# The cast ahead of a one-column product, placed earlier in a written order of the attention stage

## The chip, the cores and the metric

The kernel runs on one core of one Trainium2 chip. The metric is the device time of one execution in microseconds (us), as the median of several runs; lower is better. The engines of the core are TensorE (PE in the profile, its weight loads PEld), VectorE (DVE), ScalarE (ACT), GpSimd (POOL) and SyncE (SP), which here only issues DMAs. Each engine takes its own list of instructions in order; they meet through semaphores.

## What is computed

One layer of a decoder trunk on a sequence of 1024 positions with model width 1024, all in float32 at the interface. Cut to what matters:

```python
h = rms_norm(x, norm_mix_pre)
q, k, v, cb, cc, cx, g_att, g_conv = split(h @ w_in)       # 8 heads x 64, conv width 512
o = stick_breaking_attention(q, k, v)                      # strictly causal
y_att = o @ w_att_branch
y_conv = (cb * causal_dwconv(cc * cx, conv_mix_w)) @ w_conv_branch
merged = sigmoid(g_att) * y_att + sigmoid(g_conv) * y_conv
x = x + rms_norm(merged @ w_out, norm_mix_post)
h = rms_norm(x, norm_ffn_pre)
a, g = split(causal_dwconv(h @ w_up, conv_ffn_w))          # 2 x 2816
x = x + rms_norm((gelu(g) * a) @ w_down, norm_ffn_post)
```

The attention is, for each query t and key s < t, `w[t, s] = sigmoid(z[t, s]) * prod over s < j < t of (1 - sigmoid(z[t, j]))` with `z = q.k / 8`, and `o = w @ v`.

## The kernel before

**Products in halves.** Each operand of a large product is split into two float16 parts, a high one and the remainder, and three of the four partial products are accumulated (`PASSES`). Before it is split, an operand is scaled by a power of two that is taken from its mean square. That scale is made in these steps: ACT squares the tile and sums each partition (`sumsq`, L57); DVE casts the 128 sums to bfloat16 (`scale_sum`, L76, or L73 and L74 where several sums are added first); PE multiplies a matrix of ones with that one column (L79), which puts the total on all partitions; DVE turns the total into the power and its inverse with three integer operations (`scale_pow`, L86, L88, L89); ACT writes the high part (L192 or L96) and DVE the low part (L197 or L97).

**The stages.** After the normalisation and transposition of x come the products for v, q0 and k0, then the attention stage; then the rest of the branches, the gates, the output projection and the feed-forward part. The attention stage alone is written under a manual schedule for PE, ACT, DVE and SP: the instructions stand on each engine in the order in which the Python code issues them. The order of the other parts is planned by the compiler's own scheduler.

**The attention stage.** It walks over 24 units: four pairs of heads j, four pairs of query tiles p, and for p of 2 or 3 two ranges of keys. A unit is named j_p_first key tile (0_3_4 is j = 0, p = 3, keys from tile 4 on). Each unit has two halves, one per query tile, of a width W of 128 to 512 keys. For each half, in this order: PE makes the scores z (L510, with a mask product L514 in the range at the diagonal); ACT takes two sigmoids of them (`R` L518, `be` L519); ACT and DVE turn the weights of the half before into two float16 parts (L548, L550), which SP sends through a transposing DMA (L553); DVE runs two scans (L531) and the weighing (L540). At every second half PE also makes the weighted sums of the unit before the last one (`products`, L576).

Behind each half stands filler work for PE: 384 groups of three products of 512 columns, from v_tile (4 tiles of 8 groups), q and k of j + 1 (16 groups each, two half tiles of 8), the conv tiles (48 groups: cc, cx and cb), the two first gates (16 each) and four branch tiles (8 each). `run_fill` (in `mixer`) issues them up to a number that grows with the share of the attention that is done, some 10 groups behind a half of width 512, 7, 5 and 3 behind the narrower ones. The half tiles' PSUM comes from a pool of three buffers (`pm`), from which the one-column product takes its buffer too; the scores have two (`z`).

**The planned steps.** `plan_weight` hangs the steps of a weight's preparation on the filler's count: a step with `lead` stands so many groups ahead of the weight's first use `at`, but not ahead of its `floor`. `run_fill` calls the steps of a count just ahead of that group. Steps at count -1 are called ahead of all. In the kernel before, `total` holds both the cast and the one-column product; `split` holds the power and the high part; `low` the low part. `plan_p` does the same for the four tiles of the conv branch's product, whose squares are summed together. Weights are staged in four buffers (`ws`) from `fetch` to `low`.

Of the kernel before, what the change touches and what calls it, by code (L numbers as in the profile page):

```python
# [38 lines left out]
class Layer:  # L39
# [18 lines left out]

    def scale_of(self, sm, n, keep=False, slack=0):

        return self.scale_pow(*self.scale_sum(sm, n, keep), slack)

    def scale_sum(self, sm, n, keep=False):

        nc = self.nc
        if keep:
            r = self.const.tile([P, 4], F32, tag=f"sc{self.nsc}", name=f"sc{self.nsc}", bufs=1)
        else:
            r = self.smp.tile([P, 4], F32, tag="sc", name=f"sc{self.nsc}", bufs=16)
        self.nsc += 1  # L70
        rb = self.smp.tile([P, 1], BF16, tag="rb", name=f"rb{self.nsc}", bufs=8)
        if n > 1:
            nc.vector.tensor_reduce(r[:, 0:1], sm[:, 0:n], AX.X, ALU.add)  # L73
            nc.vector.tensor_copy(rb, r[:, 0:1])  # L74
        else:
            nc.vector.tensor_copy(rb, sm[:, 0:1])  # L76
        pool, shape, tag = self.sum_psum
        ps = pool.tile(shape, F32, tag=tag, name=f"pr{self.nsc}")
        nc.tensor.matmul(ps[:, 0:1], self.ones, rb, start=True, stop=True)  # L79
        return r, ps  # L80

    def scale_pow(self, r, ps, slack=0):
# [89 lines left out]
    def plan_weight(self, steps, name, at):  # L172

        nc = self.nc
        src = dict(self.wseq)[name][0]
        h = {}

        def fetch():
            h["sm"] = self.small(f"sm_{name}", w=8)
            h["t"] = self.ws.tile([P, D], F32, tag="ws", name=f"ws_{name}")  # L180
            nc.sync.dma_start(h["t"], src)

        def squares():
            self.sumsq(h["t"], h["sm"][:, 0:1], name)

        def total():
            h["r"], h["ps"] = self.scale_sum(h["sm"], 1)

        def split():
            h["s"], inv = self.scale_pow(h["r"], h["ps"])  # L190
            w = self.wh.tile([P, 2, D], F16, tag="wh", name=f"wh_{name}")
            nc.scalar.activation(w[:, 0, :], h["t"], AF.Copy, scale=h["s"])  # L192
            self.wdone[name] = [w], inv

        def low():
            w = self.wdone[name][0][0]
            nc.vector.scalar_tensor_tensor(w[:, 1, :], h["t"], h["s"], w[:, 0, :], ALU.mult, ALU.subtract)  # L197
        for f, lead, floor in ((fetch, 46, -1), (squares, 36, 5), (total, 30, 11), (split, 25, 15), (low, 21, 18)):
            steps.setdefault(max(floor, at - lead), []).append(f)

    def rstd_of(self, src, name):
# [108 lines left out]
    def mixer(self, mid):  # L310
        tc, nc, a = self.tc, self.nc, self.a
        hT = self.hp.tile([P, 2, KD, T], F16, tag="hT", name="hT")
        with ExitStack() as ph1:
# [66 lines left out]
            acts, inv_x = [None, o16], [None, inv_ov]  # L380
# [4 lines left out]
            smp_ = self.small("sm_p", keep=True)  # L385
# [50 lines left out]
            def plan_p(steps, at):  # L436

                h = {}
                acts[0] = []

                def total():
                    h["r"], h["ps"] = self.scale_sum(smp_, 4, keep=True)

                def power():
                    h["s"], inv_x[0] = self.scale_pow(h["r"], h["ps"])

                def part(j):
                    def f():
                        t = self.slot([P, 2, T], F16, f"p16_{j}")
                        self.split(t, pf[j], h["s"], f"p{j}")  # L450
                        acts[0].append(t)
                    return f
                for f, q in [(total, 5), (power, 10)] + [(part(j), 12 + 4 * j) for j in range(4)]:
                    steps.setdefault(at + q, []).append(f)

            sig = {}
# [36 lines left out]
            def units_of():  # L493

                for j in range(4):
                    for p in range(4):
                        for lo in ((512, 0) if p >= 2 else (0,)):
                            yield dict(j=j, p=p, lo=lo, nb=min(4, 2 * p + 2 - lo // P), nm=f"{j}_{p}_{lo // P}",
                                       top=lo > 0 or p < 2, end=lo == 0)

            def scores(u, tt, tl):

                j, i, lo, nm = u["j"], tt, u["lo"], f"{u['nm']}{tl}"
                s = stk[j]
                W = min(NH, (i + 1) * P - lo)
                z = pat.tile([P, 2, NH], F32, tag="z", name=f"z{nm}", bufs=2)
                for n, (hq, hk) in enumerate(PASSES):
                    for h in range(2):
                        d = ds(64 * h, 64)
                        nc.tensor.matmul(z[:, h, :W], s["q"][d, hq, ds(i * P, P)], s["k"][d, hk, ds(lo, W)],  # L510
                                         start=n == 0, stop=n == 2 and not u["top"], skip_group_check=True)
                if u["top"]:
                    for h in range(2):
                        nc.tensor.matmul(z[:, h, W - P:W], self.identb, self.maskb, start=False, stop=True,  # L514
                                         skip_group_check=True)
                R = att.tile([P, 2, NH + 1], F32, tag="R", name=f"R{nm}", bufs=4)
                be = att.tile([P, 2, NH], F32, tag="be", name=f"be{nm}", bufs=2)
                nc.scalar.activation(R[:, :, :W], z[:, :, :W], AF.Sigmoid, scale=s["cz"][1])  # L518
                nc.scalar.activation(be[:, :, :W], z[:, :, :W], AF.Sigmoid, scale=s["cz"][0])  # L519
                return dict(u=u, tl=tl, W=W, R=R, be=be, nm=nm)  # L520
# [16 lines left out]
            def weigh(t):  # L537

                W = t["W"]
                nc.vector.tensor_tensor(t["be"][:, :, :W], t["be"][:, :, :W], t["R"][:, :, 1:W + 1], ALU.mult)  # L540

            def turn(t, part):

                u, W, be = t["u"], t["W"], t["be"]
                w = t["R"].rearrange("p h s -> p (h s)").bitcast(F16)[:, :4 * W]
                wv = [w[:, ds(2 * W * hl, 2 * W)].rearrange("p (h s) -> p h s", h=2) for hl in range(2)]
                if part == 0:
                    nc.scalar.activation(wv[0], be[:, :, :W], AF.Copy)  # L548
                else:
                    nc.vector.tensor_tensor(wv[1], be[:, :, :W], wv[0], ALU.subtract)  # L550
                    if "wT" not in u:
                        u["wT"] = att.tile([P, 32, P], F16, tag="wT", name=f"wT{u['nm']}", bufs=2)
                    nc.sync.dma_start_transpose(u["wT"][:, ds(t["tl"] * 4 * u["nb"], 4 * W // P), :], w)  # L553
# [55 lines left out]
            def run_fill(upto):  # L609

                while state["done"] < upto:
                    for f in steps.pop(state["done"], ()):
                        f()
                    next(chained, None)
                    state["done"] += 1

            def attention():
                us = list(units_of())
                total = sum(3 * u["nb"] + 1 + (3 * min(u["nb"], 2 * u["p"] + 1 - u["lo"] // P) + 1) for u in us)
                seen, last = 0, None  # L620
                for f in steps.pop(-1, ()):
                    f()
                for k in range(len(us) + 2):
                    for tl in (1, 0):
                        if k < len(us):
                            u = us[k]
                            t = scores(u, 2 * u["p"] + tl, tl)
                            seen += 3 * (t["W"] // P) + 1
                        else:
                            t = None  # L630
                        if last is not None:
                            turn(last, 0)
                        if t is not None:
                            scan(t)
                        if last is not None:
                            turn(last, 1)
                        if t is not None:
                            weigh(t)
                        last = t
                        if tl == 0 and k >= 2:  # L640
                            products(us[k - 2])
                        run_fill(seen * (n_fill - 24) // total + 6 * max(0, 2 * (k - len(us)) + 2 - tl))
                run_fill(n_fill)
                next(chained, None)
# [566 lines left out]
```

## Time and profile before

| | |
|---|---|
| median of 3 runs | 1489.27 us (1488.35 to 1490.51) |
| profiled execution | 1490.44 us |
| span of its trace | 1488.5 us |
| mean granted TensorE clock over the span | 0.953 |
| PE busy | 1330.4 us |
| DVE busy | 1007.1 us |
| ACT busy | 804.4 us |
| attention stage: first scores to last filler group | 72.0 to 527.0 us |

The span runs from the first to the last instruction of the trace. Busy time is that of instructions; the end of a product on PE is modelled. In the profile's rows a line number such as L79 is the line of the kernel below, `out<-in` names the tiles, and `[3.82 <-DVE rb L76]` is idle time of the engine ahead of the instruction with what ended it. The granted clock is the share of TensorE's full clock that was granted in a stretch.

### The profile page before, as it was taken

What the parts mean: (1) busy time and instruction counts of PE and PEld (TensorE: products, weight loads), DVE (VectorE), ACT (ScalarE), POOL (GpSimd) and SP (SyncE); (2) the same over time, 40 slices, a digit from 0 to 9 for tenths busy, and PEclk for the clock granted to TensorE, in tenths of its full rate; (3) what the DMA queues carried; (4) which work ended last, traced back from release to release, by engine and by line L of the source; (5) the groups of instructions that cost most, each with busy time, mean ns of one, the idle gap of its engine ahead of it and who ended that gap; (6) DMA issues with size and microseconds to landing.
All of it is one profiled execution on the core that took longest, in us unless ns stands there. A gap on an engine that the chain in (4) does not pass through costs nothing. (4 is left out here: it accounts for less than half of the span.)

```text
span 1488.5 us, 16951 instructions
## 1 busy us (share of the span) xinstructions
PE 1330.4 (89%) x6543; PEld 600.0 (40%) x6543; DVE 1007.1 (68%) x1649; ACT 804.4 (54%) x1138; POOL 48.1 (3%) x69
## 2 busy tenths in 40 slices
PE   5978777788777887899999999999999999999997
PEld 3433333333333333344445444444444444444443
DVE  6455565566665419888778988596497388299848
ACT  6343444354444554656665647766576476376612
POOL 1000000000000000000001100001000100100001
PEclk9988888899888998999999999999999999999999
DMA  6022333333332401123324212515524713921315
GB/s 242 1 46 68 71 73 73 68 85 69 81 67 57 110 29 42 57 71 100 142 69 144 71 57 74 204 48 129 140 59 114 168 57 101 269 84 51 120 57 184
DMA packets 109392, 139.58 MB, mean 94 GB/s; under 512 B 79088, under 2 KB 79088, under 8 KB 109312
## 3 DMA queue, kind: packets, MB, share of 16 engines
q1 hardware_dynamic: 105360, 124.28, 27.9%
q0 software_dynamic: 3952, 14.23, 5.3%
q8 instruction: 51, 0.84, 0.2%
q14 instruction: 29, 0.24, 0.1%
HBM read 94.45 MB, written 25.17 MB: 80 GB/s over the span
## 5 line engine op out<-in xcount | busy, mean ns | idle before, releaser
L1081 PEld LDWEIGHTS <-wh_u 128*128 128x128 f16 x1848 | 178.8, 98 | 217.7 <-issue 4.0
L976 PE MATMUL pd<-wdh,f 128*128 128x512 f16 x1056 | 232.2, 381 | 10.3 <-DVE wdh L97 5.7
L976 PEld LDWEIGHTS <-f 128*128 128x128 f16 x1056 | 103.6, 98 | 137.4 <-issue 12.2
L79 PE MATMUL pr<-rb,ones 128*128 128x1 bf16 x75 | 11.9, 167 | 118.4 <-DVE rb L76 95.9
L518 ACT ACTIVATE R<-z,cz 128x1024 f32<-128x1024 f32 (+3 forms) x48 | 43.2, 899 | 114.8 <-PE z L514 59.9
L531 DVE TENSOR_TENSOR_SCAN R<-R,zero 128x256 f32<-128x256 f32 (+3 forms) x64 | 49.3, 811 | 68.0 <-ACT R L518 67.9
L1081 PEld LDWEIGHTS <-wh_g 128*128 128x128 f16 x588 | 57.0, 98 | 74.7 <-ACT hB L667 4.3
L791 PE MATMUL py<-wh_wo,m 128*128 128x512 f16 x384 | 83.9, 379 | 0.0
L97 DVE SCALAR_TENSOR_TENSOR wh_u<-ws_u,sc,wh_u 128x1024 f16<-128x1024 f32 (+1 forms) x66 | 72.2, 1102 | 8.9 <-ACT wh_u L96 8.9
L96 ACT ACTIVATE wh_u<-ws_u,sc 128x1024 f16<-128x1024 f32 (+1 forms) x66 | 64.2, 998 | 22.6 <-DVE ws_u L916 12.6
L980 ACT ACTIVATE y<-pd,sd 128x512 f32<-128x512 f32 x64 | 42.1, 692 | 58.2 <-PE pd L976 51.9
L531 DVE TENSOR_TENSOR_SCAN R<-R,cy,zero 128x512 f32<-128x512 f32 x32 | 39.4, 1272 | 40.0 <-ACT R L518 39.7
L86 DVE TENSOR_SCALAR sc<-pr 128x1 int32<-128x1 int32 x75 | 11.1, 154 | 77.0 <-PE pr L79 77.0
L1158 DVE SCALAR_TENSOR_TENSOR ugu<-cgu,cw_g,ugu 128x1023 f32<-128x1023 f32 (+1 forms) x44 | 56.3, 1280 | 10.1 <-ACT ugu L1156 10.0
L1158 DVE SCALAR_TENSOR_TENSOR ua<-cau,cw_a,ua 128x1023 f32<-128x1023 f32 (+1 forms) x44 | 56.3, 1279 | 2.0 <-ACT ua L1156 1.8
L791 PEld LDWEIGHTS <-m 128*128 128x128 f16 x384 | 37.5, 98 | 44.1
L242 PE MATMUL pcb<-hT,wh_cb 128*128 128x512 f16 x192 | 52.0, 429 | 0.0
L346 PE MATMUL pv<-wh_v,hT 128*128 128x512 f16 x192 | 48.8, 411 | 2.4 <-ACT wh_v L96 1.7
L242 PE MATMUL pcx<-hT,wh_cx 128*128 128x512 f16 x192 | 50.6, 420 | 0.0
L242 PE MATMUL pq<-hT,wh_q 128*128 128x512 f16 x192 | 48.5, 406 | 2.1 <-ACT hT L231 1.2
L242 PE MATMUL pcc<-hT,wh_cc 128*128 128x512 f16 x192 | 50.2, 420 | 0.0
L482 PE MATMUL pywa<-o,wh_wa 128*128 128x512 f16 x192 | 48.5, 416 | 1.9 <-ACT wh_wa L96 1.9
(610 smaller groups left out, 2585.0 us busy)
## 6 DMA issues: line engine op xcount, KB each, us to landing
ws_u<-w_up_nt SPq DMA_DIRECT2D x44, 512.0 KB, 3.5
yd<-y POOLq DMA_DIRECT2D x24, 512.0 KB, 5.4
ds<-w_down SPq DMA_DIRECT2D x22, 512.0 KB, 6.1
wd<-w_down SPq DMA_DIRECT2D x22, 512.0 KB, 3.5
ws_g<-w_in_nt SPq DMA_DIRECT2D x14, 512.0 KB, 3.6
x<-x SPq DMA_DIRECT2D x8, 512.0 KB, 8.1
ws_wo<-w_out SPq DMA_DIRECT2D x8, 512.0 KB, 6.4
xr<-x SPq DMA_DIRECT2D x8, 512.0 KB, 4.2
```

What stands on the lines that cost most here:

```text
L96: self.nc.scalar.activation(dst[:, 0, :], src, AF.Copy, scale=s)
L97: self.nc.vector.scalar_tensor_tensor(dst[:, 1, :], src, s, dst[:, 0, :], ALU.mult, ALU.subtract)
L242: nc.tensor.matmul(ps, w[:, wi, ds(k * P, P)], hT[:, hi, k, ds(c * NH, NH)], start=n == 0, stop=n == last)
L346: nc.tensor.matmul(pv, hT[:, hi, k, ds(tt * P, P)], wv[k // 2][:, wi, ds((k % 2) * NH, NH)], start=n == 0, stop=n == 3 * KD - 1)
L482: nc.tensor.matmul(ps, w[0][:, wi, ds((d % 2) * NH + k * P, P)], acts[bi][k][:, hi, ds(c * NH, NH)], start=n == 0, stop=n == 11)
L518: nc.scalar.activation(R[:, :, :W], z[:, :, :W], AF.Sigmoid, scale=s["cz"][1])
L531: nc.vector.tensor_tensor_scan(rev, rev, self.zero.broadcast_to([P, W]), 2.0 ** 14 if u["top"] else carry[tl][:, h, :], ALU.mult, ALU.add)
L791: nc.tensor.matmul(ps, m16[k][:, hi, ds(tt * P, P)], wo[k][:, wi, sl], start=k == 0 and p == 0, stop=k == 7 and p == 2)
L976: nc.tensor.matmul(ps, f16[g][k][:, hi, ds(tt * P, P)], w[k][:, wi, sl], start=n == 0, stop=n == 3 * GROUPS[g] - 1)
L980: nc.scalar.activation(y[:, sl], ps, AF.Copy, scale=sm[:, 0:1])
L1081: nc.tensor.matmul(ps, w[wt][:, wi, ds(wc * NH + k * P, P)], self.block(i, hi, k), start=first and n == 0, stop=n == 3 * KH - 1, skip_grou ...
L1158: nc.vector.scalar_tensor_tensor(u[:, lag:], c[:, :T - lag], sm[:, 2 - lag:3 - lag], u[:, lag:], ALU.mult, ALU.add)
```

## The change

The cast and the one-column product become two functions, and so two steps: `scale_sum` ends with the cast and returns `r, rb`; a new `scale_mm` issues the product. Where the order isn't written by hand, `scale_of` calls them one behind the other as before. In `plan_weight` and `plan_p` the steps get new places. Four filler groups are called ahead of the first unit.

```diff
     def scale_of(self, sm, n, keep=False, slack=0):
 
-        return self.scale_pow(*self.scale_sum(sm, n, keep), slack)
+        return self.scale_pow(*self.scale_mm(*self.scale_sum(sm, n, keep)), slack)
 
     def scale_sum(self, sm, n, keep=False):
...
         else:
             nc.vector.tensor_copy(rb, sm[:, 0:1])
+        return r, rb
+
+    def scale_mm(self, r, rb):
+
         pool, shape, tag = self.sum_psum
         ps = pool.tile(shape, F32, tag=tag, name=f"pr{self.nsc}")
-        nc.tensor.matmul(ps[:, 0:1], self.ones, rb, start=True, stop=True)
+        self.nc.tensor.matmul(ps[:, 0:1], self.ones, rb, start=True, stop=True)
         return r, ps
...
         def total():
-            h["r"], h["ps"] = self.scale_sum(h["sm"], 1)
+            h["r"] = self.scale_sum(h["sm"], 1)
+
+        def across():
+            h["r"] = self.scale_mm(*h["r"])
 
         def split():
-            h["s"], inv = self.scale_pow(h["r"], h["ps"])
+            h["s"], inv = self.scale_pow(*h["r"])
...
-        for f, lead, floor in ((fetch, 46, -1), (squares, 36, 5), (total, 30, 11), (split, 25, 15), (low, 21, 18)):
+        for f, lead, floor in ((fetch, 56, -1), (squares, 46, 3), (total, 40, 5), (across, 26, 13), (split, 24, 15),
+                               (low, 20, 18)):
             steps.setdefault(max(floor, at - lead), []).append(f)
...
                 def total():
-                    h["r"], h["ps"] = self.scale_sum(smp_, 4, keep=True)
+                    h["r"] = self.scale_sum(smp_, 4, keep=True)
+
+                def across():
+                    h["r"] = self.scale_mm(*h["r"])
 
                 def power():
-                    h["s"], inv_x[0] = self.scale_pow(h["r"], h["ps"])
+                    h["s"], inv_x[0] = self.scale_pow(*h["r"])
...
-                for f, q in [(total, 5), (power, 10)] + [(part(j), 12 + 4 * j) for j in range(4)]:
+                for f, q in [(total, 3), (across, 13), (power, 14)] + [(part(j), 15 + 4 * j) for j in range(4)]:
                     steps.setdefault(at + q, []).append(f)
...
                 for f in steps.pop(-1, ()):
                     f()
+                run_fill(4)
                 for k in range(len(us) + 2):
```

## The prediction

> **What bounds the kernel now.** I read the page first: the busy shares, the slices, then the costliest groups. Part 1 gives TensorE 89% of the span; the slices of part 2 show that this is no one figure. From slice 2 to slice 13 (74 to 520 us, the attention stage) PE is busy 7 to 8 tenths and its granted clock is down at 8 or 9; from slice 17 on both stand at 9.
>
> ```profile
> PE   5978777788777887899999999999999999999997
> PEclk9988888899888998999999999999999999999999
> L79 PE MATMUL pr<-rb,ones 128*128 128x1 bf16 x75 | 11.9, 167 | 118.4 <-DVE rb L76 95.9
> 72.00:527.00 455.00, 357.35 (x2010) 154.35 (x2010) 260.96 (x469) 209.15 (x282) 0.00 (x0) 0.88 0.32 71
> PE pr L79 <- DVE rb L76: 92.6, 23, 7.8
> PE pr L79 <- DVE rb L74: 5.0, 1, 5.0
> ```
>
> The third row, from the costliest groups, names the holder of the idle time: a product of one column (L79), 0.167 us each, ahead of which PE stands idle 118.4 us in all. The stage runs from the first score product at 72.0 to 527.0; its row in the view by windows (columns: us, then busy us of PE, PEld, DVE, ACT, POOL, then granted clock) gives PE 357.35 of 455.00 us. The waits of PE in that window are the last two rows: 92.6 + 5.0 = 97.6 us in 24 waits. 357.35 + 97.6 = 454.95, so PE in this stage has no idle time but this one. DVE, at 261 us, and ACT, at 209, are not full.
>
> Why the product waits is seen in the timeline of one such place:
>
> ```profile
> 78.31 0.82 PE L510 MATMUL z<-k,q 64*128 64x512 f16 x6
> 79.19 2.11 PE L346 MATMUL pv<-wh_v,hT 128*128 128x512 f16 x9
> 79.39 1.12 ACT L518 ACTIVATE R<-z,cz 128x1024 f32<-128x1024 f32 x1 [0.52 <-PE z L514]
> 80.54 2.34 DVE L531 TENSOR_TENSOR_SCAN R<-R,zero 128x512 f32<-128x512 f32 x2 [1.64 <-ACT R L518]
> 83.11 1.22 DVE L540 TENSOR_TENSOR be<-be,R 128x1024 f32<-128x1024 f32 x1
> 84.91 0.15 DVE L76 CAST rb<-sm_q 128x1 bf16<-128x1 f32 x1
> 85.11 0.16 PE L79 MATMUL pr<-rb,ones 128*128 128x1 bf16 x1 [3.82 <-DVE rb L76]
> 85.14 6.38 PE L346 MATMUL pv<-wh_v,hT 128*128 128x512 f16 x21
> L76 DVE CAST rb<-sm_cb 128x1 bf16<-128x1 f32 x4 | 0.6, 149 | 0.0
> DVE R L531 <- ACT R L518: 107.6, 37, 7.9
> ```
>
> The cast (84.91) waits for no data: the group row for it shows 0.0 idle. It stands in DVE's order behind scan and weighing of the same half, which wait for the scores that PE made just before. PE reaches the product three groups after those scores and stands until DVE has gone through. DVE in turn waits 107.6 us for ACT's sigmoids, which wait for PE: the product ties the two engines together once per weight.
>
> Each wait has a second price. After the 3.82 us wait, 21 products take 6.38 us. At full clock one costs 0.216 us: the first row below has 48 in 10.52, so (10.52 - 0.38) / 47.
>
> ```profile
> 61.53 10.52 PE L242 MATMUL pk<-hT,wh_k 128*128 128x512 f16 x48
> 105.42 0.50 PE L510 MATMUL z<-k,q 64*128 64x256 f16 x6
> 105.85 0.28 PE L514 MATMUL z<-maskb,identb 128*128 128x128 bf16 x2
> 105.97 3.40 PE L346 MATMUL pv<-wh_v,hT 128*128 128x512 f16 x15
> 109.31 0.34 PE L510 MATMUL z<-k,q 64*128 64x128 f16 x6
> 109.79 0.69 PE L576 MATMUL o<-wT,v 128*64 128x256 f16 x12
> 110.41 1.47 PE L346 MATMUL pv<-wh_v,hT 128*128 128x512 f16 x6
> 112.46 0.82 PE L510 MATMUL z<-k,q 64*128 64x512 f16 x6
> 113.22 0.82 PE L242 MATMUL pq<-hT,wh_q 128*128 128x512 f16 x3
> 232.20 0.16 PE L79 MATMUL pr<-rb,ones 128*128 128x1 bf16 x1 [2.38 <-DVE rb L76]
> 232.22 3.36 PE L242 MATMUL pk<-hT,wh_k 128*128 128x512 f16 x9
> ```
>
> What the stage would take on PE at full clock, from starts in these rows: 384 groups of 3 products, 1152 x 0.216 = 248.5. Scores: 0.76 for a half of width 512 (112.46 to 113.22), 0.55 at 256 with its mask (105.42 to 105.97), 0.48 at 128; 0.88 and 0.72 taken for 512 and 384 with a mask; 16 x 0.76 + 8 x (0.88 + 0.72 + 0.55 + 0.48) = 33.2. Weighted sums: 8 units at 0.62 (109.79 to 110.41) and 16 at twice that, 24.8. Some 0.1 at each of 48 returns to the scores (105.97 to 109.31, less 15 x 0.216), 4.8; the one-column products, 0.8. Sum **312 us**. So 357 - 312 = **45 us** of the busy time is slow clock behind the waits, and 98 us the waits.
>
> **The change, part by part.** A weight's steps are placed so many groups ahead of its use. Cast: 30 to 40 ahead; one-column product: 30 to 26; the power on DVE and high half on ACT: 25 to 24; low half: 21 to 20; fetch and squares: both 10 earlier. No instruction is added or taken away; four filler groups go ahead of the first scores.
>
> *Waits.* Between cast and product now lie 14 groups: 14 x 0.65 = 9.1 us of PE work, and one or two halves' scores. A wait is left only where DVE runs over 10 us behind PE; the waits of today, with no lead, are at most 7.8. The first two weights have 8 and 14 groups because of their floors. All 97.6 us go.
>
> *What is late next.* I followed the new written order by hand over one round of 80 groups (from unit 0_3_4 to 1_2_0), PE at full clock, DVE and ACT by these durations:
>
> ```profile
> L531 DVE TENSOR_TENSOR_SCAN R<-R,cy,zero 128x512 f32<-128x512 f32 x32 | 39.4, 1272 | 40.0 <-ACT R L518 39.7
> L550 DVE TENSOR_TENSOR R<-be,R 128x1024 f16<-128x1024 f32 x24 | 29.2, 1215 | 5.4 <-ACT R L548 5.4
> L197 DVE SCALAR_TENSOR_TENSOR wh_cx<-ws_cx,sc,wh_cx 128x1024 f16<-128x1024 f32 x4 | 5.1, 1278 | 0.5 <-ACT wh_cx L192 0.5
> L518 ACT ACTIVATE R<-z,cz 128x1024 f32<-128x1024 f32 x24 | 26.7, 1112 | 69.3 <-PE z L510 53.8 <-PE z L514 15.5
> L192 ACT ACTIVATE wh_cx<-ws_cx,sc 128x1024 f16<-128x1024 f32 x4 | 4.6, 1148 | 12.4 <-DVE sc L88 12.4
> L57 ACT ACTIVATE jk_p<-pf 128x1024 bf16<-128x1024 f32 x4 | 4.2, 1056 | 10.6 <-DVE rb L76 4.2 <-DVE sgn L100 3.8 <-DVE pf L432 2.6
> L398 ACT ACTIVATE q<-pq 128x512 f16<-128x512 f32 x6 | 3.6, 592 | 4.9 <-PE pq L242 4.9
> L399 DVE SCALAR_TENSOR_TENSOR q<-pq,q 128x512 f16<-128x512 f32 x6 | 4.1, 687 | 8.3 <-ACT q L398 8.3
> L86 DVE TENSOR_SCALAR sc<-pr 128x1 int32<-128x1 int32 x25 | 3.9, 155 | 6.9 <-PE pr L79 6.9
> DVE sc L86 <- PE pr L79: 6.9, 11, 4.3
> 551.74 0.16 DVE L76 CAST rb<-sm_wa 128x1 bf16<-128x1 f32 x1 [26.21 <-ACT jk_wa L57]
> wT<-R SPq DMA_TRANSPOSE x48, 4.2
> ```
>
> A wide half costs DVE 2 x 1.27 (scans) + 1.22 (weighing, 83.11) + 1.22 (L550) = 5.0 us, with evictions and its share of a weight (1.28 and three times 0.155 per 16 groups) about 7; PE spends 0.76 + 30 x 0.216 = 7.2, or 8.5 with a weighted sum. PE stays the slower of the two, but not by much. The filler's PSUM comes from three buffers, one of them taken by the one-column product each time: a half tile of 8 groups needs the bank of the half tile before the last one, so that one's eviction must be done 8 groups, 5.2 us of PE, after its last product. That is now the shortest leash.
>
> It snaps at the end of a conv tile. Count from the end of DVE's last eviction of pf; in my count PE came 0.6 us before that to the start of the half of unit 1_2_4 that is 128 wide. ACT: sum of squares of pf 1.06 and another weight's 1.06, both with 0.2 to read out: 2.5; a sigmoid of width 256, by its width 0.7: 3.2, its second: 3.9. DVE: the scans of that half, 1.3: 4.5; L550, held by ACT's copy: 5.7; weighing 0.7: 6.4; then the half of width 128, 0.7 + 0.7 + 0.4: 8.2; the power 0.5: 8.7; ACT's split 1.15 and its copy of q 0.59: 10.4; DVE's eviction 0.69: **11.1**. PE: scores 0.5, weighted sum 0.6 and 3 groups 1.9, from -0.6: 2.4; it waits for the score buffer until 3.9 (1.5), does 0.76 and 5 groups: 7.9, and needs the bank that is freed at 11.1 (3.2). With one wait of 0.6 earlier in the round this is **5.3 us per 80 groups**. The first 53 groups gave none; 331 / 80 x 5.3 = 22, and 3 more where the four splits of p fall together near the end: **25 us of new waits** (estimate).
>
> *Clock.* The 2.38 us wait at 232.20 is followed by 9 products in 3.36 us, where 8 x 0.216 + 0.38 = 2.1: 1.3 us lost. With about 2.8 us a round, 331 / 80 x 2.8 = **12 us stay slow of 45**. The Trainium skill (TensorE: Matmul & The Clock Gate, Part 1) speaks against counting anything here: by it the clock falls back only after an idle window of about 3.4 us, so my waits of at most 3.2 us would cost no clock and the stage 12 us shorter. The trace disagrees: 2.38 us were enough at 232.20.
>
> *The rest.* The transposes land 4.2 us after issue, and three halves lie between them and their readers: hidden. Fetches stay 10 groups ahead of their squares, on SP behind the transposes; those 10 groups shrink from 11.9 us (455 / 384 x 10) to about 9. If a fetch landed 2 us late at each of 25 weights it would cost ACT 50 us, under ACT's idle 246: none to 10 us on PE, taken as none. A staging buffer is held 36 groups instead of 25; four buffers of one weight per 16 groups give 64. DVE's power now has 2 groups behind the product instead of 5; it waits 6.9 us in 11 waits today, and when it waits, it is ahead of PE: nothing to zero. The four groups put first move the first scores 2.6 us back, and PE has no hole there: zero. Past 527 nothing moves but in time: there DVE waits for ACT's squares of the next weights.
>
> *Sum.* 312 + 25 + 12 = 349 us for the stage, against 455: 106 less. The profiled execution took 1490.4 (span 1488.5), so 1384; against the median of 1489.27 it is **1383 us**.
>
> **The rivals.**
> 1. *DVE becomes the bound.* For: 261 us of work in 349 is 75%, in strict order, with a handover to ACT in each half. If every half keeps one unhidden passage of scores and sigmoid, 48 x (0.76 + 1.11) = 90, and each of 25 weights one of ACT's split, 25 x 1.15 = 29, the stage is 261 + 119 = 380: 75 less, **1414**. Then PE would wait on the PSUM banks all over. Against: scores lie ready while DVE works on the half before.
> 2. *No leash snaps.* The stage falls near PE's 312: 143 less, **1346**. Against: the small halves above.
> 3. *The cast is late for its data, not for its place.* Then it moves and finds no squares; PE waits as before: **1489**. Against: 0.0 idle ahead of the casts.
> 4. *Slower: the shorter lead of DVE's power.* It stands 2 groups, 1.3 us, behind the product. If DVE runs ahead of PE at each of 25 places, waits as long as the longest seen, 4.3 us, and ACT's split (1.15) and the next sigmoid come as much later to PE, that is 25 x 5.45 = 136 us against the 106 gained: it breaks even at 4.2 us a place, and gives **1519** at 5.45. It decides only if DVE is both ahead of PE and bounding it, which the 11 small waits do not show.
>
> **How the numbers follow.** Forecast (1355 to 1400) 0.60; rival 1 (1400 to 1440) 0.24; rival 2 0.09; rival 3, or a small part of the gain, 0.04; rival 4 0.03. The range goes from near rival 2, **1348**, to above rival 1, **1428**. Faster by over 0.2% (3 us, about what a measurement of this kernel can tell from no change) 0.95, same 0.02, slower 0.03.
>
> **What would show it.** Right: the L79 wait in the stage under 10 us; PE busy near 320 to 330 us there, granted clock 0.96 or more; small new waits of PE on evictions of the filler (L398, L430, L432) or on scores after conv tiles. DVE's wait for sigmoids well under 107.6 us. Wrong: waits at L79 that stay; PE waits on banks over 50 us (rival 1); ACT waiting for fetches at L57; or a later part of the kernel, past the stage, that changes by more than a few us.

## The result, and the profile after

The changed kernel took **1372.36 us** (median of 4 runs, 1370.48 to 1373.79) against 1489.89 us for the kernel before beside it (4 runs, 1488.35 to 1490.95): a ratio of **0.9211**, 95% interval 0.9195 to 0.9227. The profiled execution has a span of 1371.1 us, 117.4 less than before, and a granted clock of 0.984 instead of 0.953. Line numbers move by a few: the product is L83 now, the power L90, the scores L521.

First the page's busy share of PE and, from the slices, PE and its clock; slices 2 to 11 are the attention stage now. Then the stage's row in the view by windows (columns as before).

```profile
PE 1294.1 (94%) x6543; PEld 592.0 (43%) x6543; DVE 1004.2 (73%) x1649; ACT 802.0 (58%) x1138; POOL 48.1 (4%) x69
PE   5999999999888789999999999999999999999997
PEclk9999999999999899999999999999999999999999
```

```profile
72.00:406.10 334.10, 318.34 (x2005) 145.29 (x2003) 258.03 (x469) 206.28 (x281) 0.00 (x0) 0.99 0.45 97
```

The stage ends at 406.1 instead of 527.0; from 72.0 on it takes 334.1 us instead of 455.0. (The four groups in front start 1.1 us ahead of 72.0 now, with 1.1 us of PE work; the table below counts them in, 335.2 us.) DVE and ACT do what they did (258 and 206 us). On PE two terms fell: waits from 97.6 to 334.1 - 318.3 = 15.8 us, 82 less, and busy time from 357.4 to 318.3 + 1.1 = 319.4, **38 less for the same instructions**: the clock, which in the stage went from 0.88 to 0.99. So a third of the gain is not waiting time but the slow products behind the waits.

What PE still waits for in the stage (the view of waits: total, times, longest):

```profile
PE pcc L250 <- DVE k L407: 5.1, 2, 2.9
PE pr L83 <- DVE sc L90: 3.7, 1, 3.7
PE pywc L493 <- ACT ywc L498: 3.0, 1, 3.0
PE pywc L493 <- DVE p L101: 0.9, 1, 0.9
PE pywc L493 <- ACT p L100: 0.9, 1, 0.9
PE pywc L493 <- DVE sc L90: 0.8, 1, 0.8
PE pv L354 <- DVE sc L90: 0.6, 1, 0.6
```

24 waits ahead of the one-column product have become one of 3.7 us and one of 0.3. In their place stand waits of the filler for a bank (5.1 and 0.6) and, at the end, for p's splits and the branch tiles' evictions.

The two largest, read in the timeline. First cc's second half tile at 198.84:

```profile
189.91 1.15 ACT L199 ACTIVATE wh_cx<-ws_cx,sc 128x1024 f16<-128x1024 f32 x1 [4.56 <-DVE sc L92]
190.97 0.58 ACT L406 ACTIVATE k<-pk 128x512 f16<-128x512 f32 x1
191.58 0.69 DVE L407 SCALAR_TENSOR_TENSOR k<-pk,k 128x512 f16<-128x512 f32 x1 [1.57 <-ACT k L406]
192.19 1.27 DVE L204 SCALAR_TENSOR_TENSOR wh_cx<-ws_cx,sc,wh_cx 128x1024 f16<-128x1024 f32 x1
194.45 1.46 PE L250 MATMUL pcc<-hT,wh_cc 128*128 128x512 f16 x6
198.10 0.68 DVE L407 SCALAR_TENSOR_TENSOR k<-pk,k 128x512 f16<-128x512 f32 x1
198.84 0.81 PE L250 MATMUL pcc<-hT,wh_cc 128*128 128x512 f16 x3 [2.94 <-DVE k L407]
```

PE needs the bank of k's second half, which DVE's eviction at 198.10 frees. DVE had lost 1.57 us ahead of k's first eviction: ACT did the weight's split (189.91) first, and that had waited for DVE's power. Then the wait at 358.58, ahead of p's product:

```profile
349.19 0.75 DVE L440 SCALAR_TENSOR_TENSOR pf<-pcb,cv,pf 128x512 f32<-128x512 f32 x1
350.03 1.06 ACT L57 ACTIVATE jk_p<-pf 128x1024 bf16<-128x1024 f32 x1 [4.86 <-DVE pf L440]
351.21 1.06 ACT L57 ACTIVATE jk_wc<-ws_wc 128x1024 bf16<-128x1024 f32 x1
352.27 1.09 ACT L529 ACTIVATE R<-z,cz 128x1024 f32<-128x1024 f32 x1
353.39 2.34 DVE L542 TENSOR_TENSOR_SCAN R<-R,zero 128x512 f32<-128x512 f32 x2 [3.38 <-ACT R L529]
358.30 0.16 DVE L74 CAST rb<-sc 128x1 bf16<-128x1 f32 x1
358.37 0.15 DVE L90 TENSOR_SCALAR sc<-pr 128x1 int32<-128x1 int32 x1
358.58 0.16 PE L83 MATMUL pr<-rb,ones 128*128 128x1 bf16 x1 [3.74 <-DVE sc L90]
358.60 3.55 PE L250 MATMUL pgc<-hT,wh_gc 128*128 128x512 f16 x9
359.80 0.67 ACT L477 ACTIVATE sgc<-pgc,sgn 128x512 f32<-128x512 f32 x1
```

The product reads the cast at 358.30. The row puts the wait down to L90, which ends 0.06 us later, and that fits too: L90 is the last to read the bank of the one-column product before, and the two halves of `pgc` hold the other two banks of the pool (the first is evicted at 359.80 only). So this product waited for its operand and for a bank, and both stand on DVE one behind the other. They stood late because ACT's sum of squares waited 4.86 us for DVE's last eviction of pf and did another weight's squares before the next sigmoid, so that DVE stood 3.38 us.

### The profile page after: what moved, and what is told of

Its sections match the earlier page's. It is cut to its first block, busy times and chain, and to the rows that moved or that the text cites. A ratio compares the mean times of both kernels' runs of the same rounds, so it can differ in the third digit from the quotient of the medians.

```text
span 1371.1 us, 16955 instructions
## 1 busy us (share of the span) xinstructions
PE 1294.1 (94%) x6543; PEld 592.0 (43%) x6543; DVE 1004.2 (73%) x1649; ACT 802.0 (58%) x1138; POOL 48.1 (4%) x69
## 5 line engine op out<-in xcount | busy, mean ns | idle before, releaser
L988 PE MATMUL pd<-wdh,f 128*128 128x512 f16 x1056 | 235.6, 385 | 10.1 <-DVE wdh L101 5.6
L90 DVE TENSOR_SCALAR sc<-pr 128x1 int32<-128x1 int32 x75 | 10.9, 151 | 73.1 <-PE pr L83 73.1
L250 PE MATMUL pcc<-hT,wh_cc 128*128 128x512 f16 x192 | 44.4, 386 | 5.1 <-DVE k L407 5.1
L493 PE MATMUL pywc<-p,wh_wc 128*128 128x512 f16 x192 | 42.8, 379 | 6.4 <-ACT ywc L498 3.8
L354 PE MATMUL pv<-wh_v,hT 128*128 128x512 f16 x192 | 44.4, 382 | 4.0 <-DVE r_pre L217 1.7
L57 ACT ACTIVATE jk_u<-ws_u 128x1024 bf16<-128x1024 f32 x44 | 46.4, 1055 | 2.6 <-DMA ws_u<-w_up_nt 1.9
L561 DVE TENSOR_TENSOR R<-be,R 128x1024 f16<-128x1024 f32 (+3 forms) x48 | 45.3, 944 | 2.3 <-ACT R L559 2.0
L250 PE MATMUL pq<-hT,wh_q 128*128 128x512 f16 x192 | 43.8, 379 | 2.1 <-ACT hT L239 1.2
L551 DVE TENSOR_TENSOR be<-be,R 128x1024 f32<-128x1024 f32 (+3 forms) x48 | 45.7, 952 | 0.1
```

Source lines behind the costliest of these rows:

```text
L57: self.nc.scalar.activation(self.junk(f"jk_{name}"), src, AF.Square, accum_out=acc)
L250: nc.tensor.matmul(ps, w[:, wi, ds(k * P, P)], hT[:, hi, k, ds(c * NH, NH)], start=n == 0, stop=n == last)
L493: nc.tensor.matmul(ps, w[0][:, wi, ds((d % 2) * NH + k * P, P)], acts[bi][k][:, hi, ds(c * NH, NH)], start=n == 0, stop=n == 11)
L988: nc.tensor.matmul(ps, f16[g][k][:, hi, ds(tt * P, P)], w[k][:, wi, sl], start=n == 0, stop=n == 3 * GROUPS[g] - 1)
```

## The experiments

The diffs in this section are cut to the steps that change. The theory: the distance in the written order between the cast and the product that reads it gave the gain, and DVE's lag behind PE, handed on through ACT, sets what is left. The rivals: the earlier fetches and squares, the product's later place, or the four groups in front gave it; or 14 groups are needed because the lag grows. "Stage" is from the end of k0's products to the end of the last filler group in the profiled execution; "rb" is PE's wait ahead of L83 in it. The kernel before measured 1488.5 to 1491.6 us beside them.

| kernel | us, median | ratio to before, 95% interval | stage, us | rb, us |
|---|---|---|---|---|
| before | 1489.89 | | 455.0 | 97.6 |
| changed (14 groups) | 1372.36 | 0.9211 (0.9195 to 0.9227) | 335.2 | 4.0 |
| cast 0 ahead | 1475.51 | 0.9903 (0.9883 to 0.9922) | 439.2 | 89.0 |
| both early, 0 ahead | 1480.82 | 0.9932 (0.9905 to 0.9958) | 443.4 | 90.3 |
| cast 4 ahead | 1407.34 | 0.9438 (0.9409 to 0.9467) | 371.9 | 39.5 |
| cast 8 ahead | 1373.90 | 0.9227 (0.9214 to 0.9239) | 338.8 | 8.0 |
| no groups in front | 1371.22 | 0.9204 (0.9182 to 0.9226) | 338.0 | 4.0 |
| power and splits 2 later | 1377.91 | 0.9250 (0.9237 to 0.9262) | 342.3 | 2.3 |
| splits alone 2 later | 1364.47 | 0.9155 (0.9136 to 0.9175) | 328.8 | 2.5 |
| pf's squares 4 later | 1363.98 | 0.9156 (0.9144 to 0.9169) | 326.7 | 0.3 |
| the last two together | **1359.59** | 0.9132 (0.9114 to 0.9150) | 324.2 | 0.3 |
| 61 us more on DVE | 1431.08 | 0.9609 (0.9596 to 0.9622) | 394.7 | |
| 20 us more on DVE | 1387.01 | 0.9307 (0.9294 to 0.9320) | 351.5 | |
| without the weighing | 1355.42 | 0.9092 (0.9080 to 0.9105) | 320.2 | |

**The distance taken back, in two ways.** The cast in the product's step:

```diff
-(total, 40, 5), (across, 26, 13)
+(total, 26, 13), (across, 26, 13)
-[(total, 3), (across, 13), (power, 14)]
+[(total, 13), (across, 13), (power, 14)]
```

> The changed kernel with the cast alone moved back to the step of its product (0 groups ahead instead of 14); fetch, squares, product, power, splits and the four groups in front stay where the change put them. If the distance between cast and product is what gave the gain, PE waits for rb again, 80 to 110 us in the stage, slow clock comes back, and the time is 1470 to 1500 us. If the earlier fetches and squares, the product's later place or the four groups gave it, the time stays within 10 us of 1372 us.

And the product in the cast's step, so that all is early but the distance is 0:

```diff
-(total, 40, 5), (across, 26, 13), (split, 24, 15), (low, 20, 18)
+(total, 40, 5), (across, 40, 5), (split, 35, 15), (low, 31, 18)
-[(total, 3), (across, 13), (power, 14)]
+[(total, 3), (across, 3), (power, 8)]
```

> The changed kernel with the product in the step of the cast, 40 groups ahead of the weight's use, and the power and splits as far behind it as in the kernel before (35 and 31 ahead); for p all at 3 and the power at 8. Everything is as early as in the changed kernel or earlier, only the distance is 0. If the distance gave the gain: 80 to 110 us of waits for rb, 1470 to 1500 us. If earliness against the weight's use gave it: within 10 us of 1372 us.

PE's waits from 72 to 540 us, of the first:

```profile
PE pr L83 <- DVE rb L76: 87.6, 23, 6.0
PE pr L83 <- DVE rb L74: 4.7, 1, 4.7
```

and of the second:

```profile
PE pr L83 <- DVE rb L76: 83.4, 23, 8.5
PE pr L83 <- DVE rb L74: 6.9, 1, 6.9
```

(3.3 us of the first row of the first lies past the stage.) 1475.5 and 1480.8 us: the waits are back, in 23 and 24 places, wherever the pair stands, and neither early squares nor a late product helps. Of the 117.5 us, 103 and 108 hang on the distance. What makes these two about 1% faster than the kernel before was not told apart.

**How much distance.** The cast 4 groups ahead (`total` 30, for p 9), and 8 ahead (34, for p 5):

> The changed kernel with the cast 4 groups ahead of its product instead of 14. Four groups are 2.6 us of PE. If the wait is the lag of DVE behind PE less the distance, each of the 24 waits (mean 4.1 us with no distance) keeps 1 to 2 us: 25 to 45 us of waits, and part of the slow clock: 1405 to 1445 us. If any distance that frees the cast from the half just ahead of the product is enough, 1372 to 1385 us. If 14 groups are needed because DVE's lag grows once PE runs on, over 1450 us.

> The changed kernel with the cast 8 groups ahead of its product instead of 14 (34 ahead of the use; for p from 5 to 13). 8 groups are 5.2 us of PE, and with no distance the waits were 3.6 to 3.8 us in the mean and at most 6.0 to 7.8. If the wait is DVE's lag less the distance, 2 to 12 us of waits for rb are left: 1372 to 1388 us. If only the full 14 free it, 1395 us or more.

Waits in the stage at 4 groups:

```profile
PE pr L83 <- DVE rb L76: 39.0, 17, 5.3
PE pr L83 <- DVE rb L74: 0.5, 1, 0.5
```

89.0 us at 0 groups, 39.5 at 4, 8.0 at 8, 4.0 at 14 (of the 8.0, two waits near p's splits make 6.4; of the 4.0, the wait of 3.7 shown above); the times go 1475.5, 1407.3, 1373.9, 1372.4. Four groups, 2.6 us of PE, took 2.2 us off each of 23 waits on the mean. Nearly nowhere does the lag grow to need 14: 8 do as well within the runs' scatter.

**The groups in front.** `run_fill(4)` left out:

> The changed kernel without the four filler groups ahead of the first scores. PE had no idle time there in the kernel before, so by the theory of the waits nothing changes beyond 3 us: 1369 to 1376 us. If those groups give the two first weights the time that their casts need, a wait of 2 to 5 us comes back ahead of the first two products: 1375 to 1382 us.

1371.2 us, and no wait ahead of the first two products: they give nothing.

**The order of split and eviction.** Power and high half at 22, low half at 18:

```diff
-(split, 24, 15), (low, 20, 18)
+(split, 22, 15), (low, 18, 18)
```

> The changed kernel with power and high half 22 groups ahead of the weight's use instead of 24, and the low half 18 instead of 20. At 24 the step stands ahead of the eviction of the filler's first half tile, so that ACT does the split, which waits for DVE's power, before the eviction. If the bank of a half tile is what PE waits for at the start of cc's second half (2.9 and 2.1 us), the two waits shrink to 0 to 2 us in sum, and the time falls by 2 to 6 us, to 1366 to 1371 us. If DVE's amount of work sets those waits, they stay at 4 to 5 us and the time at 1371 to 1375 us.

A miss: 5.5 us slower. PE's waits from 72 to 540 us in that run:

```profile
PE pk L250 <- DVE q L407: 3.5, 3, 2.1
PE pcc L250 <- DVE k L407: 2.8, 2, 2.5
PE pcb L250 <- DVE u L438: 1.9, 1, 1.9
PE pcc L250 <- DVE pf L440: 1.1, 1, 1.1
```

k's wait fell from 5.1 to 2.8, but waits for q's, u's and pf's evictions came, which the changed kernel has hardly any of. The power had moved too, and with it the moment at which the one-column product gives its bank back: behind the eviction of the filler's first half tile instead of ahead of it. The next run holds that fixed:

```diff
-(split, 24, 15), (low, 20, 18)
+(power, 24, 15), (split, 22, 15), (low, 18, 18)
```

> The changed kernel with the power left at 24 groups ahead and only ACT's high half (22) and DVE's low half (18) later, so that the one-column product's bank is given back as early as in the changed kernel and the eviction stands ahead of the split. If the later split at 22 lost 6 us because that bank came free two groups later, behind the eviction, so that every half tile then took the bank of a half tile whose eviction was not yet done, PE's waits for q's and u's evictions go and the time is 1366 to 1373 us. If the later splits themselves cost it, the time stays at 1376 to 1380 us.

1364.5 us, 1.5 us under the lower end of the expectation; PE's waits for q, u and pf are gone, and that for k, in the stage, is

```profile
PE pcc L252 <- DVE k L409: 1.7, 1, 1.7
```

The order of the eviction was worth 8 us, and the later return of a bank more than took it back: 13.4 us lie between the two runs. That the pool hands out the bank that was given back first fits both; it was inferred, not read from the code.

**ACT's squares at the end of a conv tile.**

```diff
-                self.sumsq(pf[j], smp_[:, j:j + 1], f"p{j}")
+                steps.setdefault(state["done"] + 4, []).append(
+                    lambda: self.sumsq(pf[j], smp_[:, j:j + 1], f"p{j}"))
-[(total, 3), (across, 13), (power, 14)]
+[(total, 5), (across, 13), (power, 14)]
```

> The changed kernel with ACT's sum of squares of pf four groups later at the end of each conv tile, so that the next half's sigmoids stand ahead of it, and the cast for p two groups later to stay behind it. If ACT's wait for DVE's last eviction of pf (16.3 us in 4) is what makes DVE late behind a conv tile, that wait of ACT falls to under 4 us and PE's wait of 3.7 us ahead of p's product to under 1.5 us: 1364 to 1370 us. If p's four splits are what holds the end of the stage, PE's waits of some 6 us in the first branch tiles stay, and the time changes by under 3 us.

ACT's wait ahead of the squares in the changed kernel, and then in this one:

```profile
ACT jk_p L57 <- DVE pf L440: 16.3, 4, 4.9
```

```profile
ACT jk_p L57 <- DVE pf L440: 2.4, 1, 2.4
```

PE's wait ahead of p's product fell from 3.7 to 0.3 us, and the time to 1364.0. Its cause is so shown. PE's waits in the branch tiles changed little, 5.2 us against 5.6: p's splits are another matter.

**Both together.**

> The sum of pf's squares four groups later, and ACT's high and DVE's low half two groups later with the power where it was. If the two act on different waits, the gains add to the 1364 us of the first: 1358 to 1364 us; if the later split loses what the order gains, 1364 to 1372 us.

1359.6 us: the fastest kernel of this study with the whole computation, 12.8 us under the changed one where the two gains of 8.4 and 7.9 would add to 16.3. Its interval overlaps those of the two alone, so that what the second step adds, 4 to 5 us in the medians, is not certain.

**DVE's work more and less.** Three more products of a small tile behind each weighing, and one; then no weighing at all:

```diff
                 nc.vector.tensor_tensor(t["be"][:, :, :W], t["be"][:, :, :W], t["R"][:, :, 1:W + 1], ALU.mult)
+                for _ in range(3):
+                    nc.vector.tensor_tensor(self.dj, self.dj, self.dj, ALU.mult)
```

> The changed kernel with three more DVE products of a 128x256 tile with itself behind each weighing, 48 x 3 x 0.4 = 58 us of DVE work in the stage whose result nothing reads. DVE would be busy 316 us of the 334 that the stage takes now. If PE is the bound and DVE has room, the time rises by under 25 us, to under 1397 us. If DVE's chain is as long as PE's already, it rises by 45 to 60 us, to 1417 to 1432 us.

> The changed kernel with one more DVE product of a 128x256 tile with itself behind each weighing, 48 x 0.42 = 20 us, a third of the run that added 61 us and took 59 us longer. If DVE's chain already sets the stage's end, the third is passed on as well: 1388 to 1395 us. If DVE has room up to some point and only the larger dose went past it, under 1380 us.

> The changed kernel without the weighing (the product of the sigmoids with the scanned remainders, 48 instructions, 45.7 us of DVE), so that the attention weights are the bare sigmoids. If DVE's chain alone sets the stage's end, the time falls by 40 us or more, to under 1332 us. If PE's own work is as long, only PE's waits of some 16 us and the slow clock behind them go: 1350 to 1360 us.

The added work in the group view of the run with three, and the stage of the run without the weighing:

```profile
L555 DVE TENSOR_TENSOR dj<-dj 128x256 f32<-128x256 f32 x144 | 60.9, 423 | 3.3
```

```profile
72.00:390.00 318.00, 314.89 (x2001) 144.71 (x2000) 217.53 (x421) 208.11 (x281) 0.00 (x0) 0.99 0.47 102
```

60.9 us of DVE cost 58.7 us, and a third of it (20.1 us) 14.6 us, 1.0 us below the expectation for "passed on" and well above "room". Without the weighing the time falls by only 16.9 us, and PE is busy 314.9 of 318.0 us. So after the change **the two chains are nearly equally long**: DVE's, work and handovers, leaves 2 to 6 us of room (60.9 less 58.7, 20.1 less 14.6), and with 45.7 us less of DVE work it is PE's own work that sets the end, 17 us earlier.

## Why the prediction was right

The forecast of 1383 us was 11 us too long; the likeliest case and its order of terms came out. By its steps:

- *The reason for the wait is place, not data* (against rival 3): right. Both runs with distance 0 bring the waits back whatever else is early.
- *"All 97.6 us go"*: 4.0 us stayed, nearly all at p's product. The bound used there, lags of at most 7.8 us against 9.1 us of distance, is what the series 0, 4, 8, 14 shows for the weights. It missed p's product, where the distance is 10 groups (3 to 13) and not 14: the cast's place is 30 products ahead, at 346.75, and the cast ended at 358.46, so that DVE was 11.7 us behind PE there.
- *PE at full clock, 312 us*: right within 2%. With almost no waits PE was busy 317.0 us over the whole stage (71.3 to 391.4) in the run without the weighing, 1.9 of it slow products by the count of the last section, which leaves 315. The weighted sums, 26.6 us from start to start instead of 24.8, are the largest part of the difference.
- *New waits, 25 us*: measured 15.8, with the 4.0 ahead of L83. The mechanism at the end of a conv tile was right, and moving the squares proved it, but the place and the size were not. The count let DVE's last eviction of pf end 0.6 us after PE had reached the small half. The timeline has PE's scores of that half 1.6 us after the end of the eviction at 167.89, a lag 2.2 us smaller:

```profile
167.15 0.74 DVE L440 SCALAR_TENSOR_TENSOR pf<-pcb,cv,pf 128x512 f32<-128x512 f32 x1
169.52 0.34 PE L521 MATMUL z<-k,q 64*128 64x128 f16 x6
176.68 3.40 PE L250 MATMUL pk<-hT,wh_k 128*128 128x512 f16 x15
177.62 0.69 DVE L407 SCALAR_TENSOR_TENSOR q<-pq,q 128x512 f16<-128x512 f32 x1 [1.57 <-ACT q L406]
```

  And k's first product (176.68) starts before q's first eviction (177.62): it did not need that bank. The fixed turn of three banks that the prediction assumed was wrong there; with the power moved behind the eviction the predicted wait for q does appear (3.5 us). What the prediction had for the end of the stage, 3 us, was 5.6 and the 3.7 at p's product.
- *12 us stay slow*: 319.4 - 312 = 7 us remained, and only some 3 of them are seen as slow products; the rest belongs to the 312. That the one term was too small and the other too large was luck in the sum. The term took 1.3 us for a wait of 2 to 3 us as certain. Of the stage's waits two show a loss: that of 3.74 us (9 products in 3.55 us where 2.1 would do), and that of 2.13 us at 268.44 (last section); those of 2.94 and 3.05 us show none. The Trainium skill (TensorE: Matmul & The Clock Gate, Part 1), by which it takes an idle window of about 3.4 us to slow the clock, came nearer in the sum here; the wait of 2.13 us disagrees with it.
- *"Past 527 nothing moves but in time"*: nearly. The rest took 3.5 us longer: the down-projection's products average 385 ns instead of 381, with slow clock in two stretches of it. One profiled execution each is too little to call that an effect of the change.
- *Rival 1*, DVE as the bound, was closer than its 0.24 and the words "scores lie ready" suggest: 20 us more on DVE already cost 15.
- *Rival 4*, the power's shorter lead: in the changed kernel DVE waits for the product once in the stage, 4.1 us. It decides nothing.

The sum by measured terms: 312 + 15.8 + 7 = 335 us against the 349 of the forecast. The stage ends 120.9 us earlier, 3.5 us are given back behind it, and the span is 117.4 us shorter.

## What to carry to other kernels

Where an order is written by hand, a tiny operation that one engine hands to another (here 0.15 us of DVE for 0.17 us of PE) costs the lag between the two engines each time, not its own duration; it should be issued ahead by more work than that lag, and the lag is read from the waits (here 8 groups, 5.2 us, were enough). An engine that is busy 77% in such a stage need not have room: its idle time can be handovers, and only work put on it or taken off shows which. In a small pool of buffers the order in which they are given back counts as much as the moment: two groups later, behind an eviction, cost more than the eviction's better place gained.

## What the runs showed of the hardware

The slow clock behind a wait depends on the wait's length, but with no sharp edge. In the stages of before, changed, both kernels with distance 0 and that with 4, over all 92 waits of PE of 0.6 us or more, the loss in the first row of products behind each was taken as its time less 0.216 us for each product but the last and 0.38 for that (a lower bound where the row is short):

| length of the wait | waits | with a loss over 0.3 us | mean loss |
|---|---|---|---|
| under 2.0 us | 24 | 0 | 0.0 us |
| 2.0 to 3.2 us | 16 | 11 | 0.8 us |
| 3.2 us and more | 52 | 51 | 1.8 us, at most 2.9 |

So 11 waits shorter than the window of about 3.4 us that the Trainium skill gives (TensorE: Matmul & The Clock Gate, Part 1) slowed the clock. The first row is not always the whole loss: one of the five others, of 2.13 us in the changed kernel, is followed by three products in 0.81 us, which is full clock, then by scores in 1.29 us instead of 0.82 and 21 products in 5.80 us instead of 4.7.

```profile
268.44 0.81 PE L250 MATMUL pcc<-hT,wh_cc 128*128 128x512 f16 x3 [2.13 <-DVE k L407]
269.18 1.29 PE L521 MATMUL z<-k,q 64*128 64x512 f16 x6
270.59 5.80 PE L250 MATMUL pcc<-hT,wh_cc 128*128 128x512 f16 x21
```

The length of one wait does not decide alone. The same wait of 3.05 us in the branch tiles costs nothing in the changed kernel and 1.6 us in that with the splits alone later:

```profile
387.48 4.04 PE L493 MATMUL pywc<-p,wh_wc 128*128 128x512 f16 x18 [3.05 <-ACT ywc L498]
```

```profile
379.13 5.64 PE L495 MATMUL pywc<-p,wh_wc 128*128 128x512 f16 x18 [3.05 <-ACT ywc L500]
```

And outside these five kernels shorter waits close together were followed by slow products too. With pf's squares later, waits of 1.46, 0.88 and 0.94 us lie within 6 us, and the 8 products behind the last take 3.29 us where 1.89 would do; in the changed kernel 0.76, 0.88 and 0.94 us at the same place cost nothing:

```profile
372.81 3.29 PE L494 MATMUL pywc<-p,wh_wc 128*128 128x512 f16 x8 [0.94 <-DVE p L101]
```

So the row under 2.0 us holds for a wait that stands alone. What else decides was not found.
